# Holding back the last second products of a feed-forward beside the next layer's attention

## The chip, the cores and the metric

The kernel runs on one core of one Trainium2 chip. A core has TensorE (matmuls), VectorE, ScalarE, GpSimd and SyncE, which issues most transfers. The metric is the device time of one execution in microseconds.

## What is computed

A trunk of two layers over 1024 tokens of width 1024, in float32. Layer 0 mixes tokens with a gated linear recurrence, layer 1 with sparse attention; each mixer is followed by a dense feed-forward, and every sub-layer has a norm with shift, scale and gate. Cut to what the change touches:

```python
# end of layer 0: its feed-forward
h = rmsnorm(x, norm_ffn_g[0]) * (1.0 + sc2) + sh2
x = x + g2 * (jnp.square(jax.nn.relu(h @ ffn_w1[0])) @ ffn_w2[0])
# start of layer 1: norm, projections, an index that picks 256 keys a query, attention over them
h = rmsnorm(x, norm_mix_g[1]) * (1.0 + sc1) + sh1
q, k, v, qi, ki, wi = jnp.split(h @ w_in, B_SPLITS, axis=-1)
q = apply_rope(rmsnorm(q.reshape(B, S, N_HEADS, HEAD_DIM), q_g), cos, sin)
```

The queries see only keys up to their own position.

## The kernel before

**Tiles and halves.** Activations stand transposed, features on the 128 partitions, in tiles of 128 x 512. A half `h` is 512 tokens; `x[h, m]` are the eight tiles of a half. For precision every operand is split in a high and a low part, and a product is three matmuls (`mm3`, L351 to L353).

**Feed-forward.** The hidden width of 4096 is cut into 16 pairs of 128 columns. `F.f1(p, h)` is the first product of a pair (48 matmuls) with its squared relu and split into hidden tiles. `F.f2([p...], h)` is the second product of one or more pairs: `f2_steps` is a generator of eight steps, one for each output tile `m`; a step accumulates over all pairs given in one PSUM bank, VectorE adds it to `x[h, m]` (L174, the eviction), and behind the last pair `tail` squares the tile for the next norm (L62, L63) and writes it out. `load1` and `load2` fetch a pair's weights. For pairs 8 to 15 both parts were kept in DRAM by the first half, so that the second half reads them back without arithmetic (L319).

**Overlap of the layers.** The first half's feed-forward ends earlier. The loop over pairs 8 to 15 of the second half (`h = 1`) has parts of layer 1's first half between its pairs, `blocks`: keys, values and index queries behind pair 8, the index scores of two token tiles behind pair 9, the first query group behind pair 13. `self.fill` holds the steps of the key choice, and `pump` runs some at each product.

**Query groups.** `q_group(h, g, ...)` projects 512 query columns for four token tiles: 96 matmuls, copies to SBUF by ScalarE (L955), a norm and the rotary turn on VectorE (L960, L965, L810 to L813), splits on ScalarE and GpSimd (L865, L866). Its transposes (`turn4`, L874, with a copy L879 on ScalarE) are put into a list and run when a score needs them. Group 0 accumulates in four `ps` banks, group 1 in two `pd` pairs.

**Norm of the next layer.** `N["m1", 1].stat()` sums the squares with eight small matmuls (L71) and makes a diagonal (L74 to L79), `bc` broadcasts it (L84, L87), `apply1(k)` makes the normed tile `hm[1][k]` in two VectorE operations and a ScalarE one (L102 to L104). Before the change this stands between the last second product and the second query group; the eight `apply1` alternate with that group's k-steps.

**Attention of the first half.** `attention(0)` goes over 16 units: four token tiles, two groups, two parities. For two heads at a time it has scores (L1124, L1125), a masked minimum on VectorE (L1136), an exponential on ScalarE (L1142), a reciprocal (L1145) and a normalisation on GpSimd (L1147); then a unit's transposes (L1152), a split of the weights (L1154, L1155) and products with the values (L1164, L1165). After each such piece it calls `mix`, which adds `rate` to an account and runs a step of a generator `background` for every whole unit in it:

```python
    def mix(self, w=1):
        self.due += w * self.rate
        while self.due >= 1 and self.bg is not None:
            self.due -= 1
            if next(self.bg, self) is self:
                self.bg = None
```

The background makes keys, values and index queries of the second half from `hm[1]` (token products, L825 to L827, three matmuls a step), reloads the first half's `x`, and begins the output projection, 32 steps, once eight units are through. `finish` runs what is left behind the last unit.

**Pools and order.** Weights have five places for high and five for low parts; a query group takes four of each, a pair of a held half one. Large tiles share 54 places, temporaries 12. `banks(True)` turns PSUM into eight single banks ahead of the attention. The order of instructions on each engine is settled when the kernel is built: program order is the priority, and an instruction that is not ready by the builder's estimate lets later ones go ahead. On the chip each engine then keeps that order.

Of the kernel before, what the change touches and what calls it, by code (L numbers as in the profile page):

```python
# [19 lines left out]
KT = 8  # L20
# [182 lines left out]
class Trunk:  # L203
# [804 lines left out]
    def topk_steps(self, t):  # L1008
# [61 lines left out]
        def ties():  # L1070
            n, e = st["n"], col("tf", FT)
            eq, run = st["eq"], st["run"] = self.wide()[:, 0:L], self.wide()[:, 0:L]
            V.tensor_scalar(eq, sc, st["v"], None, op0=OP.is_equal, op1=OP.add, accum_out=e)
            V.tensor_scalar(n, n, float(-TOPK), None, op0=OP.add)
            V.scalar_tensor_tensor(n, e, st["m"], n, op0=OP.mult, op1=OP.add)
            V.tensor_tensor_scan(run, self.ones[:, 0:1].to_broadcast([P, L]), eq, n, op0=OP.mult, op1=OP.add)
            V.scalar_tensor_tensor(eq, run, 0.0, eq, op0=OP.is_gt, op1=OP.mult)

        def fin():
            eq, run = st["eq"], st["run"]  # L1080
            V.tensor_scalar(run, sc, st["v"], BIG, op0=OP.is_lt, op1=OP.mult)
            V.scalar_tensor_tensor(sc, eq, BIG, run, op0=OP.mult, op1=OP.add)
# [175 lines left out]
    def run(self):  # L1258
        tc = self.tc
        mod = self.mod = {}  # L1260
        N = {}
        hm, hf = {}, {}

        def pool(st, name, bufs):
            return st.enter_context(tc.tile_pool(name=name, bufs=bufs))
# [8 lines left out]
        turns = []  # L1274

        def steps(fs, lag=2):

            run(feed(fs, lag))

        def run(gen):  # L1280
            for _ in gen:
                pass

        def feed(fs, lag=2):
            for f in fs:
                turns.append((yield from f()))
                while len(turns) > lag:
                    turn_next()
                yield

        def turn_next():
            for g in turns.pop(0):
                g()

        def flush():
            while turns:
                turn_next()
# [3 lines left out]
        NJ = 8  # L1301
# [11 lines left out]
        F = FFN(self, 0, None, hf)  # L1313
        with ExitStack() as st:
# [40 lines left out]
            f2 = F.f2_steps([0], 0)  # L1355
# [23 lines left out]
        with ExitStack() as st:  # L1379
            self.tp = pool(st, "tmpt", 12)  # L1380
            self.hidpool = self.tp
            self.qi, self.qiT, self.qT, self.sc = {}, {}, {}, {}
            hm[0] = []
            def start():
                N["m1", 0].bc()
                hm[0] += N["m1", 0].apply(mod[1, 1], mod[1, 0])
                self.l1_consts()

            def idx(t):
                flush()  # L1390
                for f in self.idx_steps(t):
                    f()
                self.fill += self.topk_steps(t)

            N["m1", 0].stat()
            self.npump = 2
            F.load1(NJ)
            F.f1(NJ, 1)
            start()
            blocks = [lambda: (steps(self.kv_steps(0, hm[0]), 4), steps(self.qi_steps(0, hm[0]), 4)),  # L1400
                      lambda: (idx(2), idx(3)), lambda: None, lambda: None, lambda: None,
                      lambda: (flush(), run(self.q_group(0, 0, hm[0], turns)))]
            for p in range(NJ, F.NP):
                if p + 1 < F.NP:
                    F.load1(p + 1)
                    F.f1(p + 1, 1)
                F.load2(p, 0), F.load2(p, 1)
                F.f2([p], 1)
                if blocks:
                    blocks.pop(0)()  # L1410
            self.hidpool = None
            N["m1", 1].stat()
            flush()


            self.lo = [1, 1, 0]
            q1 = self.q_group(0, 1, hm[0], self.late_turns)
            hm[1] = []
            next(q1)
            N["m1", 1].bc(keep=self.rstd_b)  # L1420
            for k in range(KT):
                hm[1].append(N["m1", 1].apply1(k, mod[1, 1], mod[1, 0]))
                next(q1)
            run(q1)
            self.drain()

            def background():
                self.second_half()
                yield from feed(self.kv_steps(1, hm[1]), 2)
                yield from feed(self.qi_steps(1, hm[1]), 2)  # L1430
                self.reload(0)
                while self.units < 8 + 1:
                    yield
                yield from self.proj_out(0, mod[1, 2], 0)

            self.banks(True)
            self.bg, self.rate = background(), 1
            self.attention(0)
            self.finish()
            flush()  # L1440
        with ExitStack() as st:
# [27 lines left out]
            F = FFN(self, 1, mod[1, 5], hf)  # L1469
# [7 lines left out]
            f2 = F.f2_steps([F.NP - 2, F.NP - 1], 0)  # L1477
# [12 lines left out]
            def background():  # L1490
# [5 lines left out]
                yield from self.proj_out(1, mod[1, 2], 0)  # L1496

            self.bg, self.rate = background(), 0.8
            self.banks(False)
            self.attention(1, before)  # L1500
# [52 lines left out]
```

## Time and profile before

| | |
|---|---|
| median of 3 runs | 2583.12 us (2579.7 to 2590.5) |
| the profiled execution | 2589.09 us |
| its span, first to last instruction | 2587.3 us |
| TensorE busy | 2449.9 us, 95% of the span |
| VectorE, ScalarE, GpSimd busy | 58%, 48%, 37% |

Matmuls are pipelined and their ends are modelled, so busy TensorE is not TensorE at its peak. Idle time of an engine that is not the bottleneck costs nothing. In the rows a time ahead of a tile or line is the start in us from the first instruction.

### The profile page before, as it was taken

The numbers are of one execution on the slowest core, as the hardware profiler recorded it, in microseconds if no ns is written. First come the engines' busy times: TensorE is split into PE (matmuls) and PEld (weight loads), VectorE is DVE, ScalarE is ACT, GpSimd is POOL, SyncE is SP. The second block draws the span as 40 slices with busy tenths as digits, with TensorE's granted clock in tenths as the row PEclk, the third lists the DMA queues.
The fourth block names the chain that finished last, engine by engine and source line by source line (L and its number), as shares of the span: only waits on it lengthen the run. The fifth ranks groups of instructions, "written<-read, shape, count | busy, mean of one in ns | idle before, by whom it ended". The sixth has DMA issues, their size and how long they took to land. (4 is left out here: it accounts for less than half of the span.)

```text
span 2587.3 us, 31024 instructions
## 1 busy us (share of the span) xinstructions
PE 2449.9 (95%) x11014; PEld 1976.0 (76%) x11014; DVE 1500.7 (58%) x2802; ACT 1234.9 (48%) x2187; POOL 965.9 (37%) x575
## 2 busy tenths in 40 slices
PE   8779899998999999999997999999998999999999
PEld 7567678776788888888776877888887777788887
DVE  3677965678934421366677877565558876321112
ACT  3455555632122142235546767768743974433322
POOL 3455421122221234230136932222225994344442
PEclk8889999999999999999998999999999999999999
DMA  6556466336611277744431431232330104322231
GB/s 207 197 183 202 164 220 227 123 110 212 207 49 49 98 249 284 279 165 175 147 117 31 172 102 57 91 97 82 105 131 8 34 25 144 111 96 92 88 101 62
DMA packets 212285, 342.53 MB, mean 132 GB/s; under 512 B 19658, under 2 KB 123298, under 8 KB 212130
## 3 DMA queue, kind: packets, MB, share of 16 engines
q1 hardware_dynamic: 183184, 295.29, 33.8%
q10 hardware_dynamic: 28946, 45.27, 5.3%
q8 instruction: 86, 1.41, 0.2%
q14 instruction: 69, 0.57, 0.1%
HBM read 274.97 MB, written 65.54 MB: 132 GB/s over the span
## 5 line engine op out<-in xcount | busy, mean ns | idle before, releaser
L334 POOL TENSOR_TENSOR wl<-raw,wh 128x1024 fp32r<-128x1024 f32 (+2 forms) x233 | 569.3, 2451 | 1102.3 <-ACT wh L328 1075.0
L328 ACT CAST wh<-raw 128x1024 fp32r<-128x1024 f32 (+2 forms) x296 | 305.5, 1035 | 599.9 <-PE ps L352 237.9
L351 PE MATMUL ps<-a,wh 128*128 128x512 f32 x1152 | 463.2, 405 | 20.3 <-DVE a L728 10.8
L352 PE MATMUL ps<-a,wh 128*128 128x512 f32 x1152 | 460.7, 400 | 1.3 <-POOL a L710 1.1
L353 PE MATMUL ps<-a,wl 128*128 128x512 f32 x1152 | 459.0, 399 | 0.8 <-DMA wl<-part 0.8
L351 PE MATMUL pd<-a,wh 128*128 128x512 f32 x1072 | 430.4, 402 | 18.8 <-DVE xc L641 14.2
L352 PE MATMUL pd<-a,wh 128*128 128x512 f32 x1072 | 430.8, 402 | 5.6 <-DVE a L100 3.6
L353 PE MATMUL pd<-a,wl 128*128 128x512 f32 x1072 | 429.9, 401 | 0.0
L174 DVE SCALAR_TENSOR_TENSOR a<-ps,mod,a 128x512 f32<-128x512 f32 x352 | 260.0, 747 | 262.3 <-PE ps L353 261.5
L351 PEld LDWEIGHTS ps<-a,wh 128*128 128x128 f32 x1152 | 219.4, 191 | 76.7 <-DVE a L728 11.4
L352 PEld LDWEIGHTS ps<-a,wh 128*128 128x128 f32 x1152 | 219.5, 191 | 55.3 <-POOL a L710 3.4
L353 PEld LDWEIGHTS ps<-a,wl 128*128 128x128 f32 x1152 | 219.1, 190 | 54.6 <-DMA wl<-part 1.6
L351 PEld LDWEIGHTS pd<-a,wh 128*128 128x128 f32 x1072 | 203.8, 190 | 69.9 <-issue 15.9
L352 PEld LDWEIGHTS pd<-a,wh 128*128 128x128 f32 x1072 | 204.8, 191 | 57.4 <-DVE a L100 4.6
L353 PEld LDWEIGHTS pd<-a,wl 128*128 128x128 f32 x1072 | 204.6, 191 | 49.3
L1147 POOL TENSOR_SCALAR s<-s,rr 128x128 f32<-128x128 f32 (+7 forms) x128 | 225.4, 1776 | 33.3 <-DVE rr L1145 30.1
L351 PE MATMUL ps<-hid,wh 128*128 128x512 f32 x512 | 205.0, 400 | 9.3 <-DVE a L174 6.5
L352 PE MATMUL ps<-hid,wh 128*128 128x512 f32 x512 | 203.9, 398 | 0.0
L353 PE MATMUL ps<-hid,wl 128*128 128x512 f32 x512 | 203.7, 398 | 0.0
L1025 ACT ACTIVATE signs<-sc,tc 128x384 int8<-128x384 f32 (+5 forms) x186 | 164.3, 884 | 77.5 <-DVE tc L1040 66.3
L458 DVE SCALAR_TENSOR_TENSOR a<-a,cond,a 128x512 f32<-128x512 f32 x140 | 134.7, 994 | 34.5 <-DMA a<-in_ada_w_dram 34.3
L152 DVE TENSOR_TENSOR a<-r,a 128x512 fp32r<-128x512 f32 x64 | 47.1, 757 | 140.2 <-ACT a L151 138.9
(275 smaller groups left out, 3750.9 us busy)
## 6 DMA issues: line engine op xcount, KB each, us to landing
raw<-in_ffn_w_dram SPq DMA_DIRECT2D x192, 512.0 KB, 3.7
a<-in_ada_w_dram ACTq DMA_DIRECT2D x160, 256.0 KB, 3.2
part<-wl SPq DMA_DIRECT2D x69, 512.0 KB, 3.1
wl<-part SPq DMA_DIRECT2D x69, 512.0 KB, 4.2
part<-wh SPq DMA_DIRECT2D x40, 512.0 KB, 4.1
wh<-part SPq DMA_DIRECT2D x40, 512.0 KB, 3.9
raw<-in_a_w_in_dram SPq DMA_DIRECT2D x34, 512.0 KB, 5.0
raw<-in_a_w_out_dram SPq DMA_DIRECT2D x20, 512.0 KB, 4.2
```

Source lines behind the costliest of these rows:

```text
L152: nc.any.tensor_tensor(ql, r, qh.bitcast(FT), op=OP.subtract)
L174: nc.vector.scalar_tensor_tensor(xt, ps, self.g2[:, m:m + 1], xt, op0=OP.mult, op1=OP.add)
L328: nc.scalar.copy(wh, raw)
L334: eng.tensor_tensor(wl, raw, wh.bitcast(FT), op=OP.subtract)
L351: pe.matmul(out, wh, xh, start=start, stop=False)
L352: pe.matmul(out, wh, xl, start=False, stop=False)
L353: pe.matmul(out, wl, xh, start=False, stop=stop)
L458: nc.vector.scalar_tensor_tensor(a, r, s, a, op0=OP.mult, op1=OP.add)
L1025: A.activation(self.signs[:, 0:L], sc, AF.Sign, bias=0.0 if neg is None else neg.bitcast(FT), accum_out=n)
L1147: G.tensor_scalar(sl[e][:, 0:L], sl[e][:, 0:L], r[:, e:e + 1], None, op0=OP.mult)
```

## The change

The second products of pairs 14 and 15 leave the loop. The loop ends with pair 13; the first product of pair 15 follows, then the first query group, which stood behind pair 13. Then a joint second product over pairs 14 and 15 is begun: its first two steps run, and the second query group follows. The other six steps, the statistic, the broadcast and the eight normed tiles become the start of the attention's background, which runs at half the rate until they are through. The hidden tiles of both held pairs come from the pool of large tiles (`hidpool = None`). The transposes of the first query group are no longer flushed ahead of the attention; a score that needs one runs it.

```diff
             blocks = [lambda: (steps(self.kv_steps(0, hm[0]), 4), steps(self.qi_steps(0, hm[0]), 4)),
-                      lambda: (idx(2), idx(3)), lambda: None, lambda: None, lambda: None,
-                      lambda: (flush(), run(self.q_group(0, 0, hm[0], turns)))]
-            for p in range(NJ, F.NP):
-                if p + 1 < F.NP:
-                    F.load1(p + 1)
-                    F.f1(p + 1, 1)
+                      lambda: (idx(2), idx(3))]
+            for p in range(NJ, F.NP - 2):
+                if p + 1 == F.NP - 2:
+                    self.hidpool = None
+                F.load1(p + 1)
+                F.f1(p + 1, 1)
                 F.load2(p, 0), F.load2(p, 1)
                 F.f2([p], 1)
                 if blocks:
                     blocks.pop(0)()
-            self.hidpool = None
-            N["m1", 1].stat()
+            F.load1(F.NP - 1)
+            F.f1(F.NP - 1, 1)
             flush()
 
 
+            run(self.q_group(0, 0, hm[0], turns))
+            f2 = F.f2_steps([F.NP - 2, F.NP - 1], 1, load=True)
+            next(f2), next(f2)
             self.lo = [1, 1, 0]
-            q1 = self.q_group(0, 1, hm[0], self.late_turns)
+            run(self.q_group(0, 1, hm[0], self.late_turns))
             hm[1] = []
-            next(q1)
-            N["m1", 1].bc(keep=self.rstd_b)
-            for k in range(KT):
-                hm[1].append(N["m1", 1].apply1(k, mod[1, 1], mod[1, 0]))
-                next(q1)
-            run(q1)
             self.drain()
 
             def background():
+                yield from f2
+                N["m1", 1].stat()
+                yield
+                N["m1", 1].bc(keep=self.rstd_b)
+                yield
+                for k in range(KT):
+                    hm[1].append(N["m1", 1].apply1(k, mod[1, 1], mod[1, 0]))
+                    yield
+                self.rate = 1
                 self.second_half()
                 yield from feed(self.kv_steps(1, hm[1]), 2)
                 yield from feed(self.qi_steps(1, hm[1]), 2)
...
             self.banks(True)
-            self.bg, self.rate = background(), 1
+            self.bg, self.rate = background(), 0.5
             self.attention(0)
             self.finish()
             flush()
```

## Rows read from the trace of the kernel before

**Rows 1.** The page, parts 1 and 2: busy time of the engines; clock in 40 slices.

```profile
PE 2449.9 (95%) x11014; PEld 1976.0 (76%) x11014; DVE 1500.7 (58%) x2802; ACT 1234.9 (48%) x2187; POOL 965.9 (37%) x575
...
PEclk8889999999999999999998999999999999999999
```

**Rows 2.** Stretches: length, busy us of each engine (instructions), clock, DMA share, GB/s.

```profile
1310.50:1366.20 55.70, 50.69 (x235) 39.83 (x234) 44.38 (x60) 27.26 (x46) 22.92 (x15) 1.00 0.31 93
1366.20:1410.00 43.80, 28.93 (x159) 24.84 (x160) 33.09 (x115) 26.53 (x82) 31.98 (x37) 0.77 0.09 22
1410.00:1515.00 105.00, 98.41 (x578) 85.20 (x577) 86.70 (x219) 81.23 (x216) 88.44 (x93) 1.00 0.46 161
1387.00:1407.50 20.50, 11.27 (x41) 7.70 (x40) 13.08 (x39) 9.49 (x27) 15.76 (x20) 0.59 0.12 26
1450.00:1475.00 25.00, 23.31 (x141) 20.57 (x140) 22.00 (x51) 19.22 (x48) 24.71 (x24) 1.00 0.41 148
1580.00:1605.00 25.00, 25.00 (x108) 20.13 (x107) 15.93 (x33) 18.62 (x36) 5.12 (x2) 1.00 0.19 64
2010.00:2035.00 25.00, 24.42 (x153) 20.61 (x154) 22.57 (x49) 23.48 (x49) 25.00 (x13) 1.00 0.05 12
```

**Rows 3.** Waits of TensorE in A and B: total us, times, longest.

```profile
PE ps L825 <- DVE mn L1136: 4.4, 1, 4.4
...
PE ps L351 <- DVE a L174: 2.9, 2, 1.6
PE ps L71 <- DVE nl L63: 2.1, 1, 2.1
...
PE ps L1124 <- ACT q L955: 1.3, 1, 1.3
```

**Rows 4.** Timelines of VectorE and GpSimd, rotary work of the second query group.

```profile
1391.84 0.68 DVE L813 TENSOR_TENSOR q<-q,a 128x512 f32<-128x512 f32 x1
...
1394.83 2.78 POOL L866 TENSOR_TENSOR a<-q,a 128x256 fp32r<-128x256 f32 x4
```

**Rows 5.** Timeline of TensorE, first score and first matmul behind the attention.

```profile
1367.45 0.33 PE L1124 MATMUL ps<-a,a 128*128 128x128 f32 x1 [1.26 <-ACT q L955]
...
1515.16 0.50 PE L351 MATMUL ps<-a,wh 128*128 128x512 f32 x1 [1.64 <-ACT a L1178]
```

**Rows 6.** Timeline of VectorE from the last eviction to the last normed tile.

```profile
1338.93 0.68 DVE L63 TENSOR_TENSOR nl<-nl,ns 128x512 f32<-128x512 f32 x1
1339.53 0.74 DVE L174 SCALAR_TENSOR_TENSOR a<-ps,mod,a 128x512 f32<-128x512 f32 x1
...
1345.28 0.88 DVE L79 TENSOR_SCALAR nl<-ident,rs 128x128 f32<-128x128 f32 x4 [1.13 <-POOL rs L76]
1348.90 2.08 DVE L102 SCALAR_TENSOR_TENSOR ns<-a,mod,rstd_b 128x512 f32<-128x512 f32 x3 [2.75 <-ACT rstd_b L87]
...
1356.48 1.90 DVE L104 SCALAR_TENSOR_TENSOR a<-ns,mod,a 128x512 fp32r<-128x512 f32 x1
...
1360.29 1.62 DVE L104 SCALAR_TENSOR_TENSOR a<-ns,mod,a 128x512 fp32r<-128x512 f32 x2
```

**Rows 7.** GpSimd: timeline beside the normed tiles; groups by shape in B.

```profile
1355.90 1.93 POOL L334 TENSOR_TENSOR wl<-raw,wh 128x656 fp32r<-128x656 f32 x1 [10.66 <-ACT wh L328]
...
L1147 POOL TENSOR_SCALAR s<-s,rr 128x512 f32<-128x512 f32 x16 | 25.4, 1601 | 6.8 <-DVE rr L1145 6.8
...
L1147 POOL TENSOR_SCALAR s<-s,rr 128x128 f32<-128x128 f32 x16 | 11.6, 743 | 9.4 <-DVE rr L1145 9.4
```

**Rows 8.** The page, parts 5 and 6: GpSimd's split of weights; reads of ready parts.

```profile
L334 POOL TENSOR_TENSOR wl<-raw,wh 128x1024 fp32r<-128x1024 f32 (+2 forms) x233 | 569.3, 2451 | 1102.3 <-ACT wh L328 1075.0
...
wl<-part SPq DMA_DIRECT2D x69, 512.0 KB, 4.2
```

**Rows 9.** The second layer's held steps: the stretch; timeline of ScalarE.

```profile
1966.20:1992.00 25.80, 20.11 (x92) 15.64 (x91) 21.67 (x42) 7.90 (x20) 9.47 (x9) 0.99 0.00 1
...
1990.55 2.04 ACT L879 CAST a<-ps 128x512 fp32r<-128x512 f32 x4
```

## The prediction

> **What bounds the kernel now.** I read the page first: the TensorE row and the clock row [rows 1]. Matmuls fill 95% of the span, so a change pays only through time in which TensorE is idle or runs at the lower clock, and the clock row has one run of dips behind the middle. Then the table of stretches [rows 2]. The change touches two. A, 1310.5 to 1366.2, holds the second products of the last two pairs and the second query group: TensorE busy 50.69 of 55.70, so 5.0 idle. B, 1366.2 to 1515, is the first attention: busy 28.93 of 43.80 and then 98.41 of 105.00, so 14.9 and 6.6 idle. At B's start the granted clock also falls: 0.59 on the mean from 1387 to 1407.5, a mix of the two levels. TensorE is busy 11.27 there; at 0.59 some 82% of the stretch is at the lower level, so about 9.2 of these us ran at half speed and 4.6 are lost by it. Together 31 us can be had at most; 19.5 of them lie in the 44 us at the start of the attention.
>
> The waits of TensorE [rows 3] say who is late: VectorE in every large one. In A it is the eviction of a second product (2.9) and the sums of squares ahead of the norm (2.1), in B the masked minimum (4.4), beside smaller ones; the change of PSUM pool waits 1.3 for a ScalarE copy. Why VectorE is late at B's start is in [rows 4]: the rotary work of the second query group, whose last matmul ends with A, is through on VectorE only at 1392.5 (1391.84 + 0.68), and GpSimd's last split of it at 1397.6 (1394.83 + 2.78). GpSimd is busy 31.98 of these 43.80 us [rows 2]. So B starts as a jam of VectorE and GpSimd, with little for TensorE beside it (token products of the second half).
>
> **The change part by part.** One second-product step is 12 matmuls over two pairs. A stretch of nothing but matmuls shows 108 in 25 us [rows 2], 0.2315 each. So a step is 2.8 us; eight steps are 96 matmuls, as many as now.
>
> *A.* What stays there behind the first query group: two steps (24 matmuls) and the second query group (96): 120 × 0.2315 = 27.8 us. VectorE holds up little in it: only two evictions mix with the first group's rotary work, there are four banks for them, and the statistic is gone. I take 28 for 55.7, **-27.7**. Of this 5.0 is idle time removed; the rest is work that goes to B: six steps (16.7), 32 transposes of the first group that were flushed at the end of A and now come unit by unit (about 3), the statistic and broadcast (about 1).
>
> *B.* The background now yields half as often at first. Counted in the code, the attention has 110 turns of the background. The six steps fall on turns 2 to 12, the statistic on 14, the broadcast on 16, the eight normed tiles on 18 to 32; only then the token products, 72 turns that began at turn 1 before. About 4 of the 32 output-projection yields still fit; 28 (84 matmuls, 19.5 us) run behind the last unit, beside the tail. That covers the wait of 1.64 for ScalarE ahead of the next stage [rows 5].
>
> What is new on B's engines is VectorE's work, step by step from [rows 6]: six evictions at 0.745 = 4.5; six sums at 0.68 = 4.1; the statistic's four diagonals, 0.88, with one small operation 1.0; 16 operations of the normed tiles at 0.745 = 11.9. Sum 21.5. Eight evictions fewer (two pairs share one) are saved in A, where they no longer matter. ScalarE gets 8 casts, 6 squares and 9 copies of the same size; at VectorE's 0.745 each that is 17 us (an estimate) on 26.53 + 81.23 of 148.8, and it stays behind VectorE. GpSimd gets one power and the contention below.
>
> That contention is a row [rows 6]: a normed tile's second operation starts at 1356.48 and takes 1.90 instead of 0.74, while GpSimd's subtraction runs from 1355.90 to 1357.83 [rows 7]; it ends 0.55 behind it, its own work still to do. VectorE waited for GpSimd. The operations at stake read two SBUF tiles: 16 + 6 = 22. In B GpSimd mostly normalises; the smallest form takes 0.74, the largest 1.60 [rows 7]. Bounds: 0 each, or the 1.16 of that row each (25 us). I take 0.14, 3 us in all, since the rotary operations among these same normalisations took 0.68 at 1391.84 [rows 4], as if alone. So VectorE in B: 33.09 + 86.70 = 119.8 now, 119.8 + 21.5 + 3 = 144.3 after.
>
> TensorE in B: 28.93 + 98.41 - 4.6 + 16.7 + 4 = 143.4. So VectorE and TensorE come out level, and neither fills a stretch in which they feed each other through eight PSUM banks. What share VectorE reaches decides B's length. Now it is 119.8 of 148.8, 0.805, with the jam inside; in the best stretch of the same attention 22.00 of 25, 0.88; in the second attention 22.57 of 25, 0.90 [rows 2]. I take 0.87, nearest to the best stretch, since the six steps cover the start: 144.3 / 0.87 = 166, **+17**. Bounds 0.92 (157, +8) and 0.805 (179, +30.5).
>
> That leaves TensorE some 23 us short in B, less than the 31 of now. Where: 1.3 at the change of pools, untouched. Some 4 at the jam: it lasts 31 us from the last query matmul (1366.2 to 1397.6), the steps cover 16.7 of it and the first units most of the rest. Then a new gap: from the last eviction to the first normed tile the chain takes 1348.90 - 1340.27 = 8.6 us, all eight end at 1361.9, 21.6 in all [rows 6]. Until the first tile TensorE has only the attention's narrow units, and behind it three short matmuls a tile. I put 12 there, the rest as now.
>
> Weights: the held halves come as ready high and low parts, 512 KB each, 4.2 us to landing at the median [rows 8], two pairs times two parts times two halves, on SyncE's queue as now. The first half's two pieces of each kind stay in use beside the second group's four; five places a kind mean that its last piece waits until the first two k-steps are over (24 matmuls, 5.6 us), is needed four k-steps later (another 48, 11.1 us), and needs one cast and one subtraction, which takes 2.5 [rows 8]; with as much for the cast 5: not late. What is queued behind on SyncE are the second half's parts, needed after the third and fourth steps; the DMA share in B's start is 0.09 [rows 2], so at nothing. If GpSimd were late with it, the second group would wait 2 to 3 us. The hidden tiles of both pairs move to the larger pool; no row shows its free places: taken at nothing, bound 3 us.
>
> **Sum.** -27.7 + 17 = -10.5, say -10. The profiled execution took 2589.1 (span 2587.3), so 2579 for one like it. It lies 6 above the median of the runs, 2583.1, so the forecast there is **2573**; own range 2566 to 2581. Half a per cent is 12.9 us, about what a measurement of this kernel can tell from no change (the three runs span 10.8): the likeliest case is inside it.
>
> **Rivals.**
> *Fill (0.25).* The scheduler lets later units and token products run in the gap behind the steps and VectorE reaches 0.92: B is 157, sum -19.7, 2563. For it: the second attention runs at 24.42 of 25 with VectorE at 22.57 [rows 2]. Against: its units are wider, and VectorE stands above 0.90 in no stretch of an attention read here.
>
> *The jam stays (0.13).* VectorE keeps 0.805 over the longer stretch: B 179, sum +2.8, 2586. For it: the work added stands in one dependent chain.
>
> *Steps ahead, not beside (0.10).* The second layer holds back steps in the same way, and there [rows 9] the last matmul of its second query group was followed by 5.7 us idle in 25.8 and 92 matmuls, 72 of them steps by the code's count; the copies that the first score needs ran on ScalarE only at 1990.55, 24 us after the group. If that happens here, the 16.7 us of steps still hide a rotary chain of that length, but the attention starts some 24 us later, without its jam: 24 + 148 now from the first score on [rows 5], less 15 of the jam, plus the gap of 12 and 3 of contention, 172, sum -4.5; with the 5.7 idle as there about 0: 2583.
>
> *Slower (0.10).* Each of the 22 two-input operations finds GpSimd at work and waits. At 1450 to 1475 GpSimd is busy 24.71 of 25 [rows 2], so the chance that it is at work is high. At the bound of 1.16 each, VectorE has 141.3 + 25.5 = 166.8, B is 192, sum +15, 2598. It decides (over 12.9 slower) from 1.07 a piece on. The Trainium skill states such a rule in SBUF — State Buffer, Who interferes with whom: the second read path is shared, the first to start keeps it for its whole instruction and the other is blocked. The row at 1356.48 agrees with it, the one at 1391.84 shows no wait; by the rule alone every meeting would cost up to a whole normalisation. Against this rival: the wait ends with GpSimd's piece, on the mean half of one.
>
> My forecast has the remaining 0.42. Faster by over 0.5%: a quarter of my own range's chance and nearly all of Fill, 0.36. Slower by over 0.5%: most of the last rival and a tail, 0.10. Within: 0.54. Range: down past Fill's 2563 by 6, up to 2592, short of the last rival; it leaves out under 0.2.
>
> **What would show it.** Right: no wait for an eviction or a sum of squares ahead of the attention; the second query group without a gap; step matmuls among the first scores; the clock high through the jam; a new idle stretch of TensorE of about 12 us ahead of the first token product, ended by VectorE's normed tile; the output projection behind the last unit without the 1.64 wait. Wrong: normed-tile operations of 1.5 us and more (slower), 72 step matmuls in a row and a late first score (steps ahead), or TensorE busy over 0.9 from the first score on (fill). The prediction fails altogether if the held tiles block a pool and a query product or a first product waits for a place.

## The result and the profile after

The changed kernel takes 2613.5 us (median of 4 runs, 2611.5 to 2616.0) where the kernel before took 2585.7 beside it: ratio 1.0097, 95% interval 1.0080 to 1.0114. The forecast was 2573, so the prediction was wrong, in sign and outside its range.

The page of the changed kernel, to be held against [rows 1]: busy time of TensorE, and the clock in 40 slices.

```profile
PE 2455.6 (94%) x11014; PEld 1983.5 (76%) x11014; DVE 1501.7 (57%) x2794; ACT 1232.0 (47%) x2187; POOL 963.5 (37%) x575
...
PEclk7889999999999999999988899999998999999999
```

Busy time is nearly the same on all engines: VectorE 1501.7 against 1500.7, TensorE 2455.6 against 2449.9. TensorE's 5.7 are for the same 11014 matmuls, at a mean granted clock of 0.966 against 0.974. So the change added next to no work; of the 25.2 us that the span grew, 19.5 are idle time of TensorE. Four starts on TensorE, read from its timeline, divide the region from the second query group to the stage behind the attention. The changed kernel (start, duration; in brackets the idle time before and what ended it):

```profile
1336.31 0.40 PE L949 MATMUL pd<-wh,a 128*128 128x512 f32 x1
1338.01 0.85 PE L874 MATMUL ps<-identR,a 128*128 128x128 f32 x8 [1.30 <-ACT q L955]
1358.73 0.48 PE L1124 MATMUL ps<-a,a 128*128 128x128 f32 x1 [19.88 <-ACT a L879]
...
1360.29 0.42 PE L1125 MATMUL ps<-a,a 128*128 128x128 f32 x1
1360.50 0.73 PE L351 MATMUL ps<-a,wh 128*128 128x512 f32 x1
...
1518.76 0.51 PE L1165 MATMUL ps<-pl,Vt 128*128 128x512 f32 x1
...
1540.85 0.39 PE L993 MATMUL ps<-a,a 128*128 128x512 f32 x1
```

and the kernel before, whose first score is in [rows 5]:

```profile
1365.81 0.39 PE L949 MATMUL pd<-wh,a 128*128 128x512 f32 x1
...
1512.42 0.47 PE L1165 MATMUL ps<-pl,Vt 128*128 128x512 f32 x1
...
1517.11 0.63 PE L993 MATMUL ps<-a,a 128*128 128x512 f32 x1
```

| | before | changed | difference |
|---|---|---|---|
| last matmul of the second query group (L949) | 1365.81 | 1336.31 | -29.5 |
| from it to the first score (L1124) | 1.64 | 22.42 | +20.8 |
| first score to last product with the values (L1165): "the attention" | 144.97 | 160.03 | +15.1 |
| from there to the next stage's first index score (L993): "the tail" | 4.69 | 22.09 | +17.4 |
| sum | | | +23.7 |

The spans differ by 25.2 (2612.5 - 2587.3), so 1.5 lie elsewhere. Positions of single executions wander: the second query group ends at 1365.81 in the kernel before but at 1371.15 in e5 below, and at 1336.31 in the changed kernel but at 1329.40 in e14, though these edits lie behind it. So the first row holds to 5 to 7 us. Two rows of the table, the wait and the tail, are new losses; neither stood in the forecast's sum.

**The wait ahead of the first score.** The 32 transposes of the first query group are no longer flushed; the first score runs eight of them at 1338.01, and then needs ScalarE's copy (L879). ScalarE's timeline shows where that copy stands:

```profile
1339.35 0.75 ACT L328 CAST wh<-raw 128x656 fp32r<-128x656 f32 x1
1348.69 0.71 ACT L865 CAST a<-q 128x256 fp32r<-128x256 f32 x2 [8.59 <-DVE q L813]
...
1357.48 0.71 ACT L865 CAST a<-q 128x256 fp32r<-128x256 f32 x2 [2.22 <-DVE q L813]
1358.10 1.06 ACT L879 CAST a<-ps 128x512 fp32r<-128x512 f32 x2
```

It is queued behind the splits (L865) of the second query group, each of which waits for VectorE's rotary work. ScalarE is busy for 5.45 of the 20.70 us from 1338.00 on (below), and two copies take 1.06, but the order is fixed. The held steps do not fill the wait: in TensorE's order they stand behind the first scores (1360.50, the first L351).

**The tail.** Stretches of the changed kernel (length, busy us and instructions of TensorE, its weight loads, VectorE, ScalarE, GpSimd; clock, DMA share, GB/s):

```profile
1300.00:1338.00 38.00, 36.71 (x158) 29.25 (x157) 23.64 (x41) 14.05 (x27) 14.17 (x11) 1.00 0.34 110
1338.00:1358.70 20.70, 0.85 (x8) 0.71 (x8) 18.33 (x35) 5.45 (x14) 7.90 (x9) 0.56 0.07 16
1358.70:1519.20 160.50, 136.72 (x746) 117.38 (x747) 120.10 (x320) 109.49 (x298) 115.54 (x123) 0.89 0.21 71
1390.00:1420.00 30.00, 21.64 (x110) 16.59 (x111) 24.45 (x53) 21.99 (x52) 15.44 (x16) 0.77 0.10 33
...
1519.20:1540.80 21.60, 21.60 (x104) 17.63 (x103) 10.20 (x13) 6.87 (x13) 1.71 (x4) 1.00 0.88 335
```

and of the kernel before:

```profile
1367.40:1512.90 145.50, 126.72 (x731) 109.56 (x731) 118.41 (x332) 104.51 (x290) 120.42 (x128) 0.93 0.35 119
1512.90:1517.10 4.20, 2.52 (x14) 1.81 (x13) 0.69 (x1) 2.76 (x8) 1.73 (x4) 0.96 0.44 142
```

Behind the last unit stand about 104 matmuls where there were 14: 87 of them make output-projection steps (29 of three matmuls, where before there were 2 that need the last unit) and 16 are short transposes. They run without a gap, so TensorE looks perfect there, but 27 of these steps stood between the units before. In the attention itself TensorE does 746 matmuls instead of 731 and takes 15 us more.

### The profile page after: what moved, and what is told of

It is laid out like the page before. It is cut to its first block, busy times and chain, and to the rows that moved or that the text cites. A ratio compares the mean times of both kernels' runs of the same rounds, so it can differ in the third digit from the quotient of the medians.

```text
span 2612.5 us, 31012 instructions
## 1 busy us (share of the span) xinstructions
PE 2455.6 (94%) x11014; PEld 1983.5 (76%) x11014; DVE 1501.7 (57%) x2794; ACT 1232.0 (47%) x2187; POOL 963.5 (37%) x575
## 5 line engine op out<-in xcount | busy, mean ns | idle before, releaser
L351 PE MATMUL ps<-a,wh 128*128 128x512 f32 x1184 | 477.2, 406 | 16.8 <-DVE a L728 10.4
L352 PE MATMUL ps<-a,wh 128*128 128x512 f32 x1184 | 474.8, 401 | 1.2 <-POOL a L710 1.1
L353 PE MATMUL ps<-a,wl 128*128 128x512 f32 x1184 | 473.5, 400 | 0.7 <-DMA wl<-part 0.7
L351 PE MATMUL pd<-a,wh 128*128 128x512 f32 x1072 | 430.2, 402 | 18.6 <-DVE xc L641 13.4
L174 DVE SCALAR_TENSOR_TENSOR a<-ps,mod,a 128x512 f32<-128x512 f32 x344 | 254.4, 747 | 267.8 <-PE ps L353 267.4
L351 PEld LDWEIGHTS ps<-a,wh 128*128 128x128 f32 x1184 | 226.7, 192 | 73.9 <-DVE a L728 11.2
L352 PEld LDWEIGHTS ps<-a,wh 128*128 128x128 f32 x1184 | 226.7, 191 | 56.6 <-POOL a L710 3.4
L353 PEld LDWEIGHTS ps<-a,wl 128*128 128x128 f32 x1184 | 226.2, 191 | 56.1 <-DMA wl<-part 1.5
L351 PEld LDWEIGHTS pd<-a,wh 128*128 128x128 f32 x1072 | 204.0, 191 | 69.2 <-issue 14.9
L351 PE MATMUL ps<-hid,wh 128*128 128x512 f32 x480 | 192.4, 401 | 7.2 <-DVE a L174 3.9
L353 PE MATMUL ps<-hid,wl 128*128 128x512 f32 x480 | 191.4, 399 | 0.0
L352 PE MATMUL ps<-hid,wh 128*128 128x512 f32 x480 | 191.4, 399 | 0.0
```

Source lines behind the costliest of these rows:

```text
L174: nc.vector.scalar_tensor_tensor(xt, ps, self.g2[:, m:m + 1], xt, op0=OP.mult, op1=OP.add)
L351: pe.matmul(out, wh, xh, start=start, stop=False)
L352: pe.matmul(out, wh, xl, start=False, stop=False)
L353: pe.matmul(out, wl, xh, start=False, stop=stop)
```

## The experiments

All times are ratios to the kernel before beside them, with 95% intervals. "Attention" and "tail" are the two rows of the table above, in us, read in the same way from the profiled execution; its time can lie off the median (in e5 by 7 us, in e4 by 5).

| run | ratio | attention | tail |
|---|---|---|---|
| before | 1 | 145.0 | 4.7 |
| changed | 1.0097 [1.0080, 1.0114] | 160.0 | 22.1 |
| transposes ahead (e1) | 1.0075 [1.0060, 1.0091] | 165.2 | 23.6 |
| before, no flush (e2) | 1.0036 [1.0023, 1.0049] | 139.7 | 4.6 |
| transposes behind (e3) | 1.0092 [1.0078, 1.0105] | 151.8 | 24.0 |
| e1 at full rate (e4) | 1.0073 [1.0057, 1.0088] | 179.5 | 10.0 |
| before, late products (e5) | 1.0082 [1.0069, 1.0095] | 142.3 | 23.6 |
| e1, idle VectorE work (e6) | 1.0094 [1.0080, 1.0107] | 171.6 | 23.9 |
| before, norm beside (e7) | 1.0058 [1.0046, 1.0071] | 153.3 | 12.1 |
| none held (e8) | 1.0038 [1.0025, 1.0051] | 149.9 | 5.8 |
| e1, catching up (e9) | 1.0037 [1.0024, 1.0049] | 177.7 | 4.8 |
| e1, idle GpSimd work (e10) | 1.0114 [1.0100, 1.0127] | 173.7 | 24.1 |
| before, rotary later (e11) | 1.0030 [1.0017, 1.0043] | 153.5 | 4.5 |
| e11, joint last pairs (e12) | 1.0020 [1.0009, 1.0031] | 153.6 | 4.5 |
| before, GpSimd relieved (e13) | 0.9991 [0.9978, 1.0003] | 144.8 | 5.6 |
| changed, GpSimd relieved (e14) | 1.0089 [1.0072, 1.0106] | 160.2 | 21.6 |
| e9, GpSimd relieved (e15) | 1.0028 [1.0014, 1.0043] | 175.5 | 5.1 |

### The copies: e1, e2, e3

e1 flushes ahead of the second query group, e3 behind it; e2 takes the flush out of the kernel before and does nothing else.

```diff
 # e1, in the changed kernel
             self.lo = [1, 1, 0]
+            flush()
             run(self.q_group(0, 1, hm[0], self.late_turns))
 # e3, in the changed kernel
             run(self.q_group(0, 1, hm[0], self.late_turns))
+            flush()
 # e2, in the kernel before
             N["m1", 1].stat()
-            flush()
```

> The changed kernel with the first query group's transposes run just ahead of the second query group, none left to the scores. Theory C (the 19.88 us idle of TensorE ahead of the first score is the ScalarE copies of these transposes, queued behind the second group's splits): that wait is gone, 32 transposes cost some 3 us of TensorE inside the second group, and the time is 2613 - 20 + 3, about 2596, at best 2588. Rival V (VectorE's added work and the gap ahead of the first token product set the length of the attention, so that a score that comes earlier only waits later): at most 5 us less, 2608 to 2613. Rival S (VectorE waits for GpSimd in the two-input operations): no change, 2610 to 2616.

> The kernel before with one line less, the flush behind the statistic, so that the first query group's transposes are left to the scores; nothing held back. Theory C: the first score waits until the second group's splits are through on ScalarE, some 25 us behind its last matmul, of which the jam at the attention's start gives back 10 to 15; 10 to 18 us slower than before, 2596 to 2604. Rivals V and S: no work is added on VectorE, so within 5 us of before, 2583 to 2591.

> The changed kernel with the first query group's transposes run just behind the second query group. Theory C: their copies still stand behind the second group's splits in ScalarE's order, so the wait stays; within 4 us of the changed kernel, 2610 to 2617. If it is only that transposes are left to the scores, and not where the copies stand, the wait goes as in the run with the transposes ahead: about 2596.

Theory C's figure for e1, 2596, was missed: e1 took 2607. Its ranges for e2 and e3 were met (2599 and 2612). e2 reproduces the wait in the kernel before, with nothing held back, and costs 0.36%, some 9 us. Its TensorE timeline:

```profile
1384.78 0.48 PE L1124 MATMUL ps<-a,a 128*128 128x128 f32 x1 [19.41 <-ACT a L879]
```

In e1 the wait is gone (the first score starts 1.65 behind the last query matmul, in e3 25.8), yet of 20.8 us only 5.7 (0.0022 x 2589) come back, near the 5 that rival V allowed, and the intervals of e1 and the changed kernel overlap. By the four starts, the second group ends 5.3 later, with the transposes and their waits in it; the attention is 5.2 and the tail 1.5 longer. The first units had run behind finished rotary work; now they share VectorE and GpSimd with it. Stretches of e2 (the first 40 us of its attention, then all of it) and of the kernel before (the first 40 us) show what that is worth:

```profile
1384.70:1424.70 40.00, 35.62 (x222) 33.66 (x223) 21.37 (x93) 29.21 (x88) 25.66 (x36) 0.84 0.06 14
1384.70:1525.00 140.30, 129.21 (x755) 114.70 (x756) 102.44 (x296) 103.64 (x286) 111.75 (x122) 0.94 0.35 120
...
1367.40:1407.40 40.00, 26.33 (x140) 22.36 (x141) 31.29 (x113) 23.59 (x73) 29.38 (x34) 0.75 0.10 24
```

With the rotary work done ahead of the first score, TensorE is busy 35.62 of the first 40 us instead of 26.33, at a clock of 0.84 instead of 0.75: the jam at the start is mostly gone. Yet the attention is only 5.2 shorter (139.7 against 145.0), although it has 16.0 us less of VectorE's work (102.44 against 118.41) and 8.7 less of GpSimd's. So the wait is one cause, shown by e2, with a net price of about 6 (e1) to 9 (e2), and it is not the larger part.

### Where the rest is: e4 to e8

e4 is e1 with the background at the full rate from the start (`self.rate = 0.5` to `1`). e5 is the kernel before with nothing but a late background:

```diff
             def background():
+                for _ in range(16):
+                    yield
+                self.rate = 1
                 self.second_half()
...
-            self.bg, self.rate = background(), 1
+            self.bg, self.rate = background(), 0.5
```

A turn is one of the 110 points at which the attention may run background steps: one step at the full rate, half a one at rate 0.5. e6 is e1 with one more line beside each of the first 16 token products; its extra operations are read by nothing:

```diff
+                            self.nc.vector.tensor_tensor(self.nshort(), self.rstd_b, self.rstd_b, op=OP.add)
```

e7 moves `bc` and the eight `apply1` of the kernel before into the background, at half the rate. e8 is e1 with the six held steps, too, run behind the second query group, and the background at the full rate:

```diff
-                yield from f2
 # ahead of background():
+            run(f2)
-            self.bg, self.rate = background(), 0.5
+            self.bg, self.rate = background(), 1
```

> Transposes ahead of the second group, and the background at the full rate from the start: steps, statistic and normed tiles on turns 1 to 16 in place of 2 to 32, token products 16 turns earlier, so that 16 more output-projection steps fit beside the units. If TensorE has too little work in the later units (the tail behind the last unit is 19 us of matmuls that VectorE and GpSimd wait through), 4 to 8 us less than with the transposes ahead alone; if VectorE's load sets the length, within 3 us of it; if the statistic's chain then stalls the units, up to 5 more.

> The kernel before, with nothing added or moved but this: the attention's background begins with 16 empty yields at half the rate, so the token products of the second half start on turn 33 in place of turn 1 (as late as in the changed kernel). Theory F (in the attention the units alone can't feed TensorE, since each is a chain through ScalarE, VectorE and GpSimd; it is the token products, wide and independent, that filled it, and the change delays them by 32 turns): slower by 10 to 20, about 2600 to 2610, with TensorE's gaps ended by several engines in turn. Rival V (VectorE's added work sets the length): none is added, within 4 us of before.

> The changed kernel with the transposes ahead of the second query group, and 16 more VectorE operations of 128 x 512, 0.68 us each, 10.9 us in all, one beside each of the first 16 token products; nothing reads them. Rival V: VectorE's work sets the length of the attention, so 10.9 / 0.87 = 12 us over the run without them, ratio to before about 1.012. Theory F: VectorE has idle time, 0 to 4 us over, ratio 1.0075 to 1.009.

> The kernel before with one part of the change alone: broadcast and the eight normed tiles leave the second query group and become the start of the background at half the rate (18 turns); second products and statistic stay. Theory F: token products 18 turns late, and VectorE's 12 us of normed tiles fall into the jam at the attention's start: slower by 8 to 15. Rival V: 12 us of VectorE work moved from under the second group (where it was hidden) into the attention, 12 / 0.87 = 14 slower too, but with VectorE at 0.87 or more of the attention; theory F has it below 0.8.

> The changed kernel with the transposes ahead, all eight steps of the joint second product run ahead of the attention (behind the second query group, beside its rotary work), and only statistic, broadcast and normed tiles in the background, at the full rate: token products start on turn 11. Theory F: the jam of the second group is covered by the steps, the products are 10 turns late: within 6 us of before, 2584 to 2596, and 10 or more under the run with six held. Rival V: VectorE's steps (8.6 us) leave the attention, 8.6 / 0.87 = 10 less as well, about 2597; told apart from F by the run with idle VectorE work added.

e5 is the run that tells most. No work is added or held, the token products only begin 32 turns later, and 0.82% are lost, some 21 us, as theory F forecast. Its stretches, attention and tail:

```profile
1372.80:1515.60 142.80, 114.20 (x640) 98.95 (x641) 110.30 (x321) 98.59 (x284) 115.13 (x127) 0.89 0.18 61
1515.60:1538.70 23.10, 23.10 (x104) 18.74 (x103) 10.15 (x13) 6.88 (x13) 1.70 (x4) 0.93 0.84 311
```

91 matmuls (731 to 640) have left the attention: 80 of the output projection, 18.5 us of TensorE at 0.2315 each, and 11 short transposes. It is only 2.7 us shorter, and the tail is 18.9 longer. So in the kernel before these matmuls cost little beside the units, which leave TensorE time that nothing else uses. The attention has a fixed number of turns, and each turn lost pushes one of its 32 output-projection steps out, once the six spare turns (110 less 72 and 32) are used up: by this count 26 steps in e5, 12 in e7 and 4 in e8, by the traces 27, 13 and 4. The two rows make 16.2 of the 21 us. The rest is not placed: this execution is e5's slowest, and its 11014 matmuls are busy 2464.0 us instead of 2449.9, at a mean granted clock of 0.968.

The others fit in part. e7 loses 18 turns and 15 us; its tail is 7.5 and its attention 8.3 longer, and its second query group ends 5.2 earlier. VectorE's share of that attention is 0.82 (125.86 of 153.70), between the marks of theory F and rival V. e8 loses 10 turns and 10 us, but its tail is only 1.1 longer and its attention 4.9, so pushing out explains little of its loss; with 2597 it lies at rival V's figure and just outside theory F's range. e6's 16 operations, 11.9 us in its trace where 10.9 were planned, cost 0.19%, 5 us, between the two theories and with an interval that overlaps e1's: VectorE is loaded, but its sum does not set the length by itself. e4 shortens the tail by 13.6, lengthens the attention by 14.3 and gains nothing. Part of that is TensorE's fixed order running into the statistic. Its waits for VectorE there, 14.0 in sum where e1 has 7.4:

```profile
PE ps L71 <- DVE nl L63: 7.8, 1, 7.8
PE ps L84 <- DVE nl L79: 6.2, 1, 6.2
```

### Catching up, and what paces the units: e9, e10, e13 to e15

e9 is e1 with `self.rate = 1.5` in place of `1` behind the normed tiles. e10 puts 7 GpSimd operations where e6 had 16 of VectorE. e13 to e15 put every fourth normalisation on ScalarE, in the kernel before, the changed kernel and e9:

```diff
+                if not wide and i0 == 2 and e == 1:
+                    A.activation(sl[e][:, 0:L], sl[e][:, 0:L], AF.Identity, scale=r[:, e:e + 1])
+                else:
                     G.tensor_scalar(sl[e][:, 0:L], sl[e][:, 0:L], r[:, e:e + 1], None, op0=OP.mult)
```

> The changed kernel with the transposes ahead, and the background at one and a half times the rate once the normed tiles are through, so that the 78 turns that are left take 117 steps and the whole output projection of the first group fits beside the units again. Theory F/T (the attention's length is set by its own chains, and the steps that were crowded out stand behind the last unit as 20 us of matmuls that nothing shares): the tail of 103 matmuls falls to about 14, and the attention grows by less than the 20 us taken from behind it, since TensorE lost 18 us in its second half: 8 to 15 less than with the transposes ahead alone, ratio to before 1.002 to 1.0045. If the units' length follows TensorE's work after all, tail and attention exchange the same 20 us: ratio 1.0065 to 1.0085.

> The changed kernel with the transposes ahead, and 7 more GpSimd operations of 128 x 512 in the form of the normalisation, 1.60 us each, 11.2 us in all, one beside every second of the first 14 token products; nothing reads them. The same load that VectorE had in the run with idle VectorE work, where the time rose by 5. If GpSimd paces the units: 8 to 11 over the run without them, ratio to before 1.0105 to 1.0118. If the units are paced by the chain through all three engines, about as much as on VectorE, 3 to 6: 1.0085 to 1.0098. If by VectorE alone: within 2.

> The kernel before, with every fourth normalisation of the first attention on ScalarE in place of GpSimd: 16 operations, some 19 us off GpSimd (75.1 us of L1147 / 4), some 9 us more on ScalarE (an estimate from its 128 x 512 exponentials and copies of 0.5 to 0.6). If GpSimd paces the units (11.2 us of idle work on it cost 10): 8 to 15 less than before, 2575 to 2582. If the chain of a unit through all engines sets the length: within 5 us of before, or slower, as ScalarE then waits for VectorE's reciprocal.

> The changed kernel, with the same normalisations on ScalarE and nothing else. If GpSimd paces the units: 8 to 15 under the changed kernel, ratio to before 1.004 to 1.0065, the wait for the copies and the tail unchanged. If the chain: 1.008 to 1.011.

> The run that catches up (transposes ahead, background at one and a half times the rate behind the normed tiles), with the same normalisations on ScalarE. If GpSimd paces the units: 8 to 15 under that run, ratio to before 0.998 to 1.0005, and over the kernel before with the same relief by what the change still costs. If the chain: within 4 us of the run that catches up, 1.002 to 1.005.

e9 brings the tail back to 4.8, for 12.5 us more of attention, and gains 0.38%, some 10 us, as expected: the tail was a real loss. Its attention:

```profile
1343.00:1521.20 178.20, 149.70 (x809) 126.61 (x810) 141.83 (x366) 115.38 (x308) 131.54 (x132) 0.92 0.32 112
```

So the matmuls taken in from the tail cost 12.5 of 18.8 us here, against 2.7 in the kernel before. And with the wait and the tail both undone, e9 is still 0.37%, 10 us, slower than the kernel before: the second query group ends 24.4 us earlier, but the attention with the held work in it is 32.8 longer. e10 cost 0.39% over e1, 10 of its planned 11.2 us, which pointed at GpSimd as the engine that paces. e13 takes that back. Its attention:

```profile
1369.60:1514.80 145.20, 129.60 (x730) 112.27 (x731) 119.19 (x332) 111.57 (x306) 101.71 (x112) 0.92 0.35 119
```

GpSimd is busy 101.71 us instead of 120.42, ScalarE 111.57 instead of 104.51, and the attention is as long as before; e14 and e15 are within 0.1% of their partners too, all three in the ranges given for the chain. So work put ahead of GpSimd's normalisations delays the units, and work moved from it to ScalarE frees nothing. Neither GpSimd's sum (e13), nor VectorE's (e2, above), nor TensorE's (e5) sets the length. What is left is the chain of a unit through several engines; that is argued by exclusion and not shown, as no run shortened the chain, and which link of it paces, these runs do not tell. e13 is also the only version that is not slower than the kernel before, and it can't be told from it.

### The rotary work: e11, e12

The forecast read the start of the attention as a jam made by the second query group's rotary work. e11 takes it out of there:

```diff
                 next(q1)
-            run(q1)
...
+                def spread(gen):
+                    for i, _ in enumerate(gen):
+                        if i % 6 == 5:
+                            next(q1, None)
+                        yield
-                yield from feed(self.kv_steps(1, hm[1]), 2)
+                yield from spread(feed(self.kv_steps(1, hm[1]), 2))
```

and e12 joins the second products of pairs 14 and 15 in their old place (`F.f2([14, 15], 1, load=True)`).

> The kernel before, with the norm and rotary part of the second query group taken out of the start of the attention and run beside every sixth token product instead (its scores come only after eight units); nothing is held back. If the 10 to 20 us that TensorE loses at the attention's start come from that rotary work standing ahead of the units on VectorE, as the prediction said: 6 to 12 less than before, 2576 to 2582. If the attention's length is set by the sum of what its engines do, the work only moves: within 4 us of before.

> As the run with the rotary work later, and the second products of the last two pairs joined in one step for each output tile, in their old place: 8 evictions of 0.745 fewer on VectorE, beside work in which TensorE lost 5 to 9 us: 0 to 4 less than that run.

Both of e11's cases missed: it is slower by 0.30%. Its profile names a new wait of TensorE:

```profile
PE ps L874 <- POOL a L866: 19.0, 5, 8.5
```

Transposes (L874), which TensorE has early in its order, now wait for splits of GpSimd that come later. The experiment moved the wait and so does not tell what the jam is worth; e2 says more on that. e12 stands 0.10% below e11, within its forecast of 0 to 4 us, but their intervals overlap.

## Why the prediction was wrong, point by point

**A, -27.7: right.** The second query group ends 29.5 us earlier, and TensorE is busy 36.71 of the 38.00 us to the first transposes. No wait for an eviction or for the squares is left ahead of the attention; the one for the squares came back inside it, as 1.8.

**New work on VectorE: right.** The 22 two-input operations took 6.2, 6.2 and 5.2 us:

```profile
L102 DVE SCALAR_TENSOR_TENSOR ns<-a,mod,rstd_b 128x512 f32<-128x512 f32 x8 | 6.2, 788 | 1.5 <-ACT rstd_b L87 1.5
L104 DVE SCALAR_TENSOR_TENSOR a<-ns,mod,a 128x512 fp32r<-128x512 f32 x8 | 6.2, 779 | 0.4 <-ACT a L103 0.3
L63 DVE TENSOR_TENSOR nl<-nl,ns 128x512 f32<-128x512 f32 x6 | 5.2, 874 | 0.2
```

Over 745 and 680 that is 8 x 0.043 + 8 x 0.034 + 6 x 0.194 = 1.8 us of waiting for GpSimd, against 3 in the sum and 25 in the rival. One operation carries most of it. VectorE's and GpSimd's timelines:

```profile
1371.19 1.81 DVE L63 TENSOR_TENSOR nl<-nl,ns 128x512 f32<-128x512 f32 x1
```

```profile
1370.86 1.60 POOL L334 TENSOR_TENSOR wl<-raw,wh 128x656 fp32r<-128x656 f32 x1
```

It ends 0.54 behind GpSimd's subtraction, as the row at 1356.48 ended 0.55 behind one [rows 6, 7]. The Trainium skill's rule (SBUF — State Buffer, Who interferes with whom) that the later of the two is blocked for the whole instruction agrees with both rows. It is not that meetings are seldom: what GpSimd runs makes the difference. VectorE's and GpSimd's timelines again, for a sum (L63) beside normalisations and for a rotary operation of the wait (L812) beside two splits:

```profile
1380.39 0.69 DVE L63 TENSOR_TENSOR nl<-nl,ns 128x512 f32<-128x512 f32 x1
...
1352.29 1.10 DVE L812 TENSOR_TENSOR q<-q,qtab 128x512 f32<-128x512 f32 x1
```

```profile
1374.28 7.59 POOL L1147 TENSOR_SCALAR s<-s,rr 128x256 f32<-128x256 f32 x8 [1.82 <-DVE rr L1145]
...
1352.11 1.87 POOL L866 TENSOR_TENSOR a<-q,a 128x256 fp32r<-128x256 f32 x2 [1.06 <-ACT a L865]
```

The sum began while a normalisation ran and took 0.69, as if alone, which the rule would not have; the rotary operation took 1.10. VectorE lost time beside GpSimd's two-input subtractions and not beside its normalisations, and in the attention GpSimd mostly normalises. The prediction's small price, set from the row at 1391.84, rested on the right row.

**The gap ahead of the first token product, 12: right in size, not in kind.** VectorE's timeline: the last held eviction, the first operation of the first normed tile and the last of the last:

```profile
1388.16 0.75 DVE L174 SCALAR_TENSOR_TENSOR a<-ps,mod,a 128x512 f32<-128x512 f32 x1 [0.16 <-PE ps L353]
...
1397.96 0.75 DVE L102 SCALAR_TENSOR_TENSOR ns<-a,mod,rstd_b 128x512 f32<-128x512 f32 x1 [1.46 <-ACT rstd_b L87]
...
1421.07 0.75 DVE L104 SCALAR_TENSOR_TENSOR a<-ns,mod,a 128x512 fp32r<-128x512 f32 x1
```

The chain takes 9.1 to the first tile's start instead of 8.6, and 32.9 to the last tile's end instead of 21.6, as it shares VectorE with the units. In 1390 to 1420 TensorE is idle for 8.4 us; at a granted clock of 0.77 some 46% of the stretch is at the lower level, so about 10 of its 21.64 busy us ran at half speed and 5 more are lost: 13.4. But the forecast had one stretch ended by a normed tile, and no wait there is; the idle time falls into seven waits, the longest for ScalarE's copies (2.4) and for VectorE's split of a unit's weights (2.3), so the size came out partly by luck.

**The transposes, "about 3": the first step that failed.** They were priced as TensorE's 32 matmuls. Their copies on ScalarE, and what is queued ahead of these, had no term: 19.88 us of wait. Net of what the finished rotary work gives back, the wait costs 6 to 9 (e1, e2). The rival "Steps ahead, not beside" named this very wait from the second layer [rows 9], but let the steps' matmuls run in it; here they stand behind the scores, and TensorE is idle.

**The tail: the second failed step, and by what the experiments give back the larger.** The text counted right: 28 of 32 output-projection steps behind the last unit, 84 matmuls, 19.5 us (27 in the trace). It then entered them only as cover for a wait of 1.64. B was sized by VectorE's work and share, which ends with the last unit; the 19.5 us of TensorE behind it are in no term. They stood beside the units, at 2.7 (e5), and now stand behind them at full price: the tail is 17.4 longer, in e5 18.9 with nothing else changed, and undoing it gains 10 (e9). The sum as written plus both missing terms is -10 + 19.9 + 17.4 = +27, and the measured medians differ by 27.8. That agreement is partly luck: it counts both terms at their face, of which e1 and e9 got back only about 6 and 10.

**B by VectorE's share, 0.87: wrong in principle.** VectorE was busy 120.10 of 160.50, 0.75, under the lower bound. No engine's sum sets this stretch: 91 matmuls taken out shorten it by 2.7 (e5), 16 us less of VectorE by 5.2 (e2), 19 us off GpSimd by nothing (e13). "What share VectorE reaches decides B's length" therefore fell. The length it gave was near by luck: the sum has 17 more for B, and without the wait the attention is 15.1 longer, but from 120.10 us of VectorE's work at 0.75 where the forecast had 144.3 at 0.87. Part of the difference, 18.33, ran in the wait.

**31 us to be had: not borne out.** No version here is faster than the kernel before, so none of it was had. That the rotary work makes the jam is borne out by e2, but not the 19.5 us put on it: without it the attention is 5.2 shorter. And e9 shows that work held beside the units is not hidden there: with wait and tail undone, 24.4 us saved ahead cost 32.8 in the attention. Why it costs more than it saved stays open.

## What to carry to other kernels

Idle time of TensorE beside a stage like this attention is a budget of turns: what is put into it pushes out what was there, and the last thing pushed out stands bare behind the stage. Before moving work into a loop's background, list what the background already held, see which of it no longer fits, and enter that at full price. And when a flush is dropped, look at the queue of every engine that the deferred work passes: two copies of together 1 us, behind another chain's waits, left TensorE idle for 20, of which 6 to 9 were lost in the end.

## Not expected of the hardware

Some 11 us of idle work on VectorE cost 5 (e6), on GpSimd 10 (e10), though the two intervals overlap a little. Yet 19 us moved off GpSimd to ScalarE (e13) brought nothing. Adding work to an engine was thus no test of what taking it away would give. And VectorE's two-input operations waited for GpSimd's subtractions (1.81 and 1.10 instead of 0.69) but not for its normalisations (0.69).
